# Moving work around the first attention head, the block norms and the first output projection in a hybrid state-space and attention layer

## The chip, the cores and the metric

The kernel runs on one core of a Trainium2 chip (trn2) as one launch. The metric is the device time of that launch in microseconds, the median of several runs. Beside it one execution was taken by the hardware profiler; its instruction trace is what the views below are read from.

The core has a matrix engine (TensorE; PE in the profile, its weight loads PEld), a vector engine (VectorE; DVE), an activation engine (ScalarE; ACT), a general one (GpSimd; POOL), and SyncE (SP), which here only issues DMAs. Each works through its own queue in order.

## The reference

One layer of a streaming encoder on 2048 tokens of width 1024, in float32. One RMS norm feeds one input projection, whose columns go to a state-space layer (512) and to attention (queries, keys, values, 8 heads of 64).

```python
h = rmsnorm(x, norm_mix_g)
proj = h @ w_in
y_ssm = s5_mixer(u_ssm, ...)              # diagonal complex scan, GELU, sigmoid gate
y_att = chunked_attention(q, k, v, bias)  # 64-token chunks, 8 chunks to the left
mixed = concat(rmsnorm(y_ssm, g_ssm), rmsnorm(y_att, g_att))
x = x + mixed @ w_out
h2 = rmsnorm(x, norm_ffn_g)
x = x + (silu(h2 @ w_gate) * (h2 @ w_up)) @ w_down
return rmsnorm(x, norm_final_g)
```

## The kernel before

Everything is kept transposed, features on the 128 partitions and tokens along the free dimension, in four token blocks (`sb`) of 512. Matmuls that must be exact are done with operands split into a high and a low part (`split`, L151: ACT copies the high part, DVE subtracts it for the low one), three matmuls for one product (`mm3`, L145).

The stages follow each other: the state-space input projection (`u_phase`, L398), with the prologue that builds the state-space matrices (`ssm_prologue`, L156) worked in between; attention with the state-space scan woven in (`att_phase`, L687); the mixing stage with the gate, the two norms and the output projection (`mix_phase`, L986); then gate and up, and down, which the change does not touch.

**What sets the order.** TensorE's instructions are issued in the order in which the program writes them (`Ordered`, L69). All other engines' instructions, and the DMAs on SP, are put in order ahead of time by the framework's scheduler: of the instructions whose inputs and buffers are ready in its own model of time, the one that stands earlier in the program goes first, so work can be placed far ahead of its position. At run time each queue is then fixed and in order. A new tile in a rotating buffer waits for the last reader of the tile before it.

**The prologue's end.** The last part of the prologue (`transposes`, L287) turns the state-space input matrices: per group of four, 8 TensorE transposes into tiles `pp`, four ACT copies (L293) and one store on POOL's queue to `bsts` (L296), in two steps each; four groups make eight steps. The list `PRO` (L44) says how many of these steps run behind each step of the first query and key projection (L928 to L930). Behind it, the weights of the first value projection are loaded and split (`next(v0)`, L932), what is left of the prologue runs, and the pools of the attention stage are opened, on the memory of the prologue's pool.

**Queries and keys.** `qk_unit` (L749) projects the queries (`c == 0`) and the keys (`c == 1`) of a pair of heads for one block. For block 0 and pair 0 both are done together (`both`). A head's 64 query rows come out on one half `a` of the partitions (L783). They are wanted on both halves, as a high part `q2h` and a low part `q2l`, because the key tile `k2` holds the key's high part on one half and its low part on the other, so that one matmul over 128 rows does two products. ACT and DVE write half `a` (L786, L787), and two DMAs on SP copy it to half `o` (L788, L789). For the very first pair the tiles are called `hi0x`, `lo0x` (head 0), `hi1x`, `lo1x` (head 1), `hi2x` and `lo2x` (the two key tiles).

**Attention steps.** There are 128 steps `s`, one for each block, pair, head and query tile `qp` of 128 tokens. Step `s` does the scores (`scores`, L840; TensorE writes the one tile `sc`, and DVE's L866 adds the bias, finds the minimum and frees it; ACT takes the exponential), the transposes of step `s`-2 (`transp`, L872), at a head's end the product with the values, and then one turn of all `Unit`s (L665): the projections of the next block, spread over a range of steps that is given relative to the block's first step `g0`, and the state-space work. A `Unit` may do its first piece `pre` steps early. The bias of a head lies in one of two tiles (`nba`, `nbb`); at `qp == 2` the next head's is loaded (L849).

**The operands of a block's projections.** `hT_unit` (L719) loads the eight 128-row tiles of the block's input (L726; one by one into `xt`, two buffers, or in pairs into `raw`, two buffers, which block 0 uses for weights), multiplies them by gain and inverse root (L744, the norm), and splits them (L745, L746). Tiles 0 to 2 (`DB`) have two sets of operand tiles and are done in steps `HTA`; tiles 3 to 7 have one set, which the last projection of the block before reads, and are done in steps `HTS`, with two steps of lead (`HTP`).

**The mixing stage's first block.** `w_out` (L1118) is a generator for two of the eight 128-row tiles of the output projection. Its first half multiplies the attention rows (24 matmuls), its second half the state-space rows, then adds the input tile `xt` (two buffers, L1123), stores the result and squares it. In block 0 the attention half is ready first. So the first halves of pairs 0 and 1 (`held`, L1203) are run ahead, one on either side of `spread` (L1206), which brings the inverse root `no` of the state-space rows onto the partitions by four transposes; their second halves and whole pairs follow (L1213). Between them stand the next block's norms, the sums behind pair 1, the spread and products behind pair 2 (L1223). The projection's results take PSUM tiles `big`, four of them.

Of the kernel before, what the change touches and what calls it, by code (L numbers as in the profile page):

```python
# [18 lines left out]
KT = D // P  # L19
# [18 lines left out]
SGB = 2  # L38
RA1, RA2 = 2, 12
QS = 4, 5, 6, 7, 0, 1, 2, 3  # L40
HTA = -12, -9
HTS = -8, -6
HTP = 2
PRO = 0, 0, 2, 2, 2, 2, 0, 0, 0  # L44
LIGHT = 0.8
SL = 1
LPH = 2
# [639 lines left out]
def att_phase(k, ident, S, aw, x0, roots):  # L687

    tc, nc, io, pfs = k.tc, k.nc, k.io, k.pfs
    with ExitStack() as cx:  # L690
# [28 lines left out]
        def hT_unit(sb, q0=0, q1=KT):  # L719
            hi, lo = hT.setdefault(sb, ([], []))  # L720
            ts = slice(sb * SB, (sb + 1) * SB)
            xts = {}

            def load(q, n=1):
                t = k.t(aw, "raw", [P, 1024], bufs=2) if n > 1 else k.t(aw, "xt", [P, SB], bufs=XB)
                nc.sync.dma_start(t[:].rearrange("p (q t) -> p q t", q=n), io["xt"][q * P : (q + n) * P, ts].rearrange("(q p) t -> p q t", p=P))  # L726
                for m in range(n):
                    xts[q + m] = t[:, m * SB : (m + 1) * SB]

            if q0 == 0:  # L730
                load(0)
                load(1)
            else:
                load(q0)
                for q in range(q0 + 1, q1, 2):
                    load(q, 2)
            for q in range(q0, q1):
                yield
                if q0 == 0 and q + 2 < q1:
                    load(q + 2)  # L740
                xt = xts[q]
                for v, n in zip(hT[sb], ("hi", "lo")):
                    v.append(k.t(aw, f"{n}{q}x" if q < DB and sb % 2 else f"{n}{q}", [P, SB], F32R)[:])
                nc.vector.scalar_tensor_tensor(xt, xt, k.gm[:, q : q + 1], S["rsn"][:, ts], op0=ALU.mult, op1=ALU.mult)  # L744
                nc.scalar.copy(hi[q], xt)  # L745
                nc.vector.tensor_tensor(lo[q], xt, f32(hi[q]), op=ALU.subtract)  # L746
            yield

        def qk_unit(sb, pr):  # L749
            ws = yield from load_ws(sb, (pr, 4 + pr))  # L750
            yield
            hi, lo = hT[sb]
            if (sb, pr) == (0, 0):
                ts = [[k.t(aw, f"{n}{q}x", [P, SB], F32R) for n, q in (("hi", hh), ("lo", hh), (("hi", "lo")[hh], 2))] for hh in range(2)]
            else:
                ts = [(k.t(aa, "q2h", [P, SB], F32R, bufs=3), k.t(aa, "q2l", [P, SB], F32R, bufs=3), k.t(aa, "k2", [P, 2 * SB], F32R, bufs=3)) for _ in range(2)]
            qk[sb, pr] = ts
            if sb > 0:
                for hh in range(2):
                    nc.sync.dma_start(f32(ts[hh][2][:, :SB]), S["k"][(sb - 1) % 2, 2 * pr + hh])  # L760
            both = (sb, pr) == (0, 0)
            pss = []
            for c in range(2):
                if c == 0 or not both:
                    cc = range(2) if both else (c,)
                    pss += [k.t(pfs, "pf", [P, 512]) for _ in cc]
                    for q in range(KT):
                        cs = slice(q * P, (q + 1) * P)
                        for m in cc:
                            wh, wl = ws[m]  # L770
                            mm3(k.ta, pss[m][:], wh[:, cs], wl[:, cs], hi[q], lo[q], q == 0, q == KT - 1)
                            if q == 2:
                                keep_w(4 * m + pr)
                        if q < KT - 1:
                            yield
                ps = pss[c]
                if sb == 0:
                    t = k.t(aa, "yt", [P, SB]) if pr else k.t(aw, "xt", [P, SB], bufs=XB)
                    nc.vector.tensor_tensor(t[:], ps[:], S["rsn"][:, :SB], op=ALU.mult)
                    ps = t  # L780
                for hh in range(2):
                    q2h, q2l, k2 = ts[hh]
                    a = slice(hh * 64, hh * 64 + 64)  # L783
                    o = slice(64 - hh * 64, 128 - hh * 64)
                    if c == 0:
                        nc.scalar.activation(q2h[a, :], ps[a, :], AF.Copy, scale=-0.125)  # L786
                        nc.vector.scalar_tensor_tensor(q2l[a, :], ps[a, :], -0.125, f32(q2h[a, :]), op0=ALU.mult, op1=ALU.subtract)  # L787
                        nc.sync.dma_start(f32(q2h[o, :]), f32(q2h[a, :]))  # L788
                        nc.sync.dma_start(f32(q2l[o, :]), f32(q2l[a, :]))  # L789
                    else:  # L790
                        nc.scalar.copy(k2[a, -SB:], ps[a, :])
                        nc.vector.tensor_tensor(k2[o, -SB:], ps[a, :], f32(k2[a, -SB:]), op=ALU.subtract)
                        if sb < NSB - 1:
                            nc.sync.dma_start(S["k"][sb % 2, 2 * pr + hh], f32(k2[:, -SB:]))
                yield
# [44 lines left out]
        def scores(st):  # L840
            sb, pr, hh, qp = st
            h = 2 * pr + hh
            if qp == 0:
                hd = st_head[sb, h] = Head()
                hd.nb = nbs.pop(h) if nbs else load_nb(h)
                hd.s = {}
                hd.p = None
            hd = st_head[sb, h]
            if qp == 2 and (sb, h) < (NSB - 1, H - 1):  # L849
                nbs[(h + 1) % H] = load_nb((h + 1) % H)  # L850
            q2h, q2l, k2 = qk[sb, pr][hh]
            k0 = max(qp, 4) if sb == 0 else qp
            nk = (qp + 5 - k0) * P
            half = nk // 2 if nk > 512 else nk
            nch = nk // half
            ps = k.t(psum2, "sc", [P, 2, 512])
            for c in range(nch):
                c0 = k0 * P + c * half + k2.shape[1] - 2 * SB
                cols = slice(c0, c0 + half)
                for n, q2 in ((0, q2h), (1, q2l)):  # L860
                    k.ta.matmul(ps[:, c, :half], q2[:, qp * P : (qp + 1) * P], k2[:, cols], start=n == 0, stop=n == 1)
            s = k.t(aa, "s", [P, 640], bufs=3)
            mn = k.t(aa, "mn", [P, 1], bufs=4)
            if (hh, qp) == (0, 0):
                sums[sb, pr] = k.t(aa, "sm", [P, 2, 4], bufs=3)
            nc.vector.tensor_tensor_reduce(  # L866
                s[:, :nk].rearrange("p (a b) -> p a b", a=nch), ps[:, :nch, :half],
                hd.nb[:, nk - 1 :: -1].rearrange("p (a b) -> p a b", a=nch), 1.0, 3e38, ALU.add, ALU.min, mn[:])
            nc.scalar.activation(s[:, :nk], s[:, :nk], AF.Exp, bias=mn[:], scale=-1.0, accum_out=sums[sb, pr][:, hh, qp : qp + 1])  # L869
            hd.s[qp] = s, k0  # L870
# [54 lines left out]
        pro = yield  # L925
        pps = k.pro_psum = tc.alloc_tile_pool(name="apro", bufs=6, space=bass.MemoryType.PSUM, reuse_waits="tile")
        next(pro)
        for n, _ in enumerate(first):  # L928
            for _ in range(PRO[n]):
                next(pro, None)  # L930
        v0 = v_unit(0, 0)
        next(v0)  # L932
        for _ in pro:
# [6 lines left out]
        sp = tc.alloc_tile_pool(name="ssm", reuse_waits="tile", bufs=1)  # L940
        psum = cx.enter_context(tc.tile_pool(name="aps", bufs=1, space=bass.MemoryType.PSUM, reuse_waits="tile"))
        psum2 = cx.enter_context(tc.tile_pool(name="aps2", bufs=1, space=bass.MemoryType.PSUM, reuse_waits="tile"))
        units = []
        for sb in range(NSB):
            g0 = sb * 32
            C = CUT if sb < NSB - 1 else CUTL
            if sb > 0:
                if DB:
                    units.append(Unit(hT_unit(sb, 0, DB), 2 + DB, g0 + HTA[0], g0 + HTA[1], 2))
                units += [Unit(hT_unit(sb, DB), 2 + KT - DB, g0 + HTS[0], g0 + HTS[1], HTP), Unit(qk_unit(sb, 0), QK_N, g0 + C[0], g0 + C[1], 3, light=LIGHT)]  # L950
            units.append(Unit(v_unit(sb, 0), V_N, g0 + C[1], g0 + C[2], 2, light=LIGHT) if sb else Unit(v0, V_N, *V0, done=1))
            for gen, n, c in ((qk_unit(sb, 1), QK_N, 2), (qk_unit(sb, 2), QK_N, 3), (v_unit(sb, 1), V_N, 4), (qk_unit(sb, 3), QK_N, 5)):
                units.append(Unit(gen, n, g0 + C[c], g0 + C[c + 1], 2, light=LIGHT) if sb else Unit(gen, n + 1, C[c], C[c + 1], 4, light=LIGHT, mid=2))
# [32 lines left out]
def mix_phase(k, S, bank):  # L986
# [3 lines left out]
    with ExitStack() as cx:  # L990
# [207 lines left out]
        for sb in range(NSB):  # L1198
# [1 line left out]
                b.m = {}  # L1200
                mixed(b, 0)
            if sb == 0:
                held = [w_out(0, b, 2 * n) for n in range(2)]  # L1203
                next(held[0])
                ps = big()
                spread(k, te, ps[:, :512], b.o[1], 0)  # L1206
                with tc.high_priority():
                    rstd2(b, 1, ps[:, :512])
                    mixed(b, 1)
                next(held[1])  # L1210
            else:
                mixed(b, 1)
            for n in range(4):  # L1213
                if n == 0 and 0 < sb < NSB - 1:
                    nxt = next_block(sb + 1)
                if sb or n > 1:
                    for _ in w_out(sb, b, 2 * n):
                        pass
                else:
                    next(held[n])  # L1220
# [516 lines left out]
```

## Time and profile before

| what | value |
|---|---|
| median of 3 runs | 2264.99 us (2262.37 to 2267.28) |
| the profiled execution | 2267.91 us |
| its span, first to last instruction | 2266.1 us |
| TensorE busy | 2165.6 us (96%) |
| VectorE busy | 1542.4 us (68%) |
| ScalarE busy | 1003.3 us (44%) |
| GpSimd busy | 351.2 us (15%) |
| mean granted TensorE clock | 0.982 |

A line of a timeline gives start and length in us, engine (SPq is SP's queue), source line, operation, out<-in by tile names, shapes, how many were merged, and in brackets the idle time before it and what ended it. The table of waits gives for a line and what it waited for the total, the number of times and the longest. The table of stretches gives for each stretch the busy time and number of instructions of each engine and the TensorE clock that was granted. A source view gives shortest, median and longest duration in ns, and the first and last start. Stages can be told by tile names: `sc`, `pt`, `pj` and `pf` belong to attention (from 138 us on), `big` to the mixing stage (from 720 us on).

### The profile page before, as it was taken

What the parts mean: (1) busy time and instruction counts of PE and PEld (TensorE: products, weight loads), DVE (VectorE), ACT (ScalarE), POOL (GpSimd) and SP (SyncE); (2) the same over time, 40 slices, a digit from 0 to 9 for tenths busy, and PEclk for the clock granted to TensorE, in tenths of its full rate; (3) what the DMA queues carried; (4) which work ended last, traced back from release to release, by engine and by line L of the source; (5) the groups of instructions that cost most, each with busy time, mean ns of one, the idle gap of its engine ahead of it and who ended that gap; (6) DMA issues with size and microseconds to landing.
All of it is one profiled execution on the core that took longest, in us unless ns stands there. A gap on an engine that the chain in (4) does not pass through costs nothing.

```text
span 2266.1 us, 30134 instructions
## 1 busy us (share of the span) xinstructions
PE 2165.6 (96%) x10632; PEld 1825.8 (81%) x10632; DVE 1542.4 (68%) x2695; ACT 1003.3 (44%) x1656; POOL 351.2 (15%) x827
## 2 busy tenths in 40 slices
PE   8988899999997899999999999999999999999997
PEld 6777788898986788778888887888888778888886
DVE  7756666556557756776766668766656477688776
ACT  5445555556557442353333335333333443353322
POOL 2246576656500000000000000000000010000000
PEclk9999999999998899999999999999999999999999
DMA  8878876666552435754556457645433395465652
GB/s 276 254 244 261 268 233 207 192 190 205 187 168 100 138 109 188 251 168 144 180 176 209 162 198 269 199 163 190 140 97 112 102 385 182 167 227 181 216 183 75
DMA packets 194903, 430.41 MB, mean 190 GB/s; under 512 B 19904, under 2 KB 38384, under 8 KB 187648
## 3 DMA queue, kind: packets, MB, share of 16 engines
q1 hardware_dynamic: 187104, 403.58, 53.8%
q0 software_dynamic: 7648, 24.92, 3.6%
q8 instruction: 83, 1.36, 0.2%
q14 instruction: 68, 0.56, 0.1%
HBM read 288.95 MB, written 131.10 MB: 185 GB/s over the span
## 4 chain that ended last, share of the span: by engine, by line
PE 78%; DMA 7%; DVE 6%; ACT 3%; issue 2%; SPq 0%; DVEq 0%; ACTq 0%
PE X L76 20%; PE ps L76 17%; PE Y L76 10%; PE pf L76 10%; PE big L76 6%; PE W L76 5%; PE pj L76 4%; PE pt L79 2%; PE sc L76 2%; DMA acc<-x 2%; DMA lo<-hc 1%; DMA xt<-in_xt 1%; DVE lo L153 1%; DMA hc<-gh 1%; DVE ptl L885 1%
## 5 line engine op out<-in xcount | busy, mean ns | idle before, releaser
L76 PE MATMUL X<-hi,c 128*128 128x512 f32 x1408 | 450.8, 391 | 7.4 <-DVE c L153 5.1
L76 PE MATMUL ps<-hd,hd 128*128 128x512 f32 (+1 forms) x1968 | 429.6, 380 | 3.0 <-DVE hd L153 2.0
L76 PEld LDWEIGHTS ps<-hd,hd 128*128 128x128 f32 x1968 | 357.5, 189 | 73.6 <-DVE hd L153 2.7
L76 PEld LDWEIGHTS X<-hi,c 128*128 128x128 f32 x1408 | 265.1, 188 | 64.1 <-DVE c L153 6.0
L76 PE MATMUL X<-lo,c 128*128 128x512 f32 x704 | 274.6, 390 | 0.0
L153 ACT CAST hd<-hd 128x1536 fp32r<-128x1536 f32 (+1 forms) x106 | 147.5, 1394 | 232.5 <-DMA hd<-hq 170.9
L76 PE MATMUL Y<-hi,c 128*128 128x512 f32 x704 | 226.0, 392 | 3.8 <-DVE c L153 2.3
L153 DVE TENSOR_TENSOR hd<-hd 128x1536 fp32r<-128x1536 f32 (+1 forms) x106 | 174.1, 1644 | 36.2 <-ACT hd L153 35.8
L153 DVE TENSOR_TENSOR c<-S,c 128x512 fp32r<-128x512 f32 x176 | 121.0, 688 | 103.6 <-ACT c L153 103.3
L1516 POOL DMA_DIRECT2D hd<-hq x7 | 5.3, 755 | 1173.2 <-PE X L76 1161.5
L1408 ACT COPY u<-X 128x512 f32<-128x512 f32 x132 | 77.4, 587 | 199.9 <-PE X L76 199.9
L153 ACT CAST c<-S 128x512 fp32r<-128x512 f32 x176 | 109.5, 622 | 122.5 <-PE Y L76 63.8
L76 PE MATMUL big<-m,woh 128*128 128x512 f32 x512 | 162.6, 399 | 0.0
L76 PEld LDWEIGHTS Y<-hi,c 128*128 128x128 f32 x704 | 133.3, 189 | 32.4 <-DVE c L153 2.8
L1550 DVE TENSOR_TENSOR acc<-acc,ps 128x512 f32<-128x512 f32 x196 | 130.2, 682 | 41.6 <-PE ps L76 41.3
L76 PEld LDWEIGHTS X<-lo,c 128*128 128x128 f32 x704 | 132.6, 188 | 27.4
L76 PE MATMUL pf<-hi,w 128*128 128x512 f32 x416 | 149.1, 410 | 0.0
L153 ACT CAST c<-raw 128x512 fp32r<-128x512 f32 x132 | 82.2, 622 | 149.1 <-PE Y L76 69.1
L76 PE MATMUL Y<-lo,c 128*128 128x512 f32 x352 | 137.7, 391 | 0.0
L885 DVE TENSOR_TENSOR ptl<-pt,pth 128x640 fp32r<-128x640 f32 (+3 forms) x152 | 98.3, 647 | 56.1 <-ACT pth L884 54.7
L869 ACT ACTIVATE s<-s,mn 128x640 f32<-128x640 f32 (+4 forms) x128 | 98.0, 765 | 64.1 <-DVE mn L866 58.1
L884 ACT CAST pth<-pt 128x640 fp32r<-128x640 f32 (+3 forms) x152 | 83.8, 551 | 85.6 <-PE pt L79 80.9
(448 smaller groups left out, 4274.1 us busy)
## 6 DMA issues: line engine op xcount, KB each, us to landing
w<-wss SPq DMA_DIRECT2D x36, 1024.0 KB, 6.2
hq<-g SPq DMA_DIRECT2D x140, 256.0 KB, 2.1
hd<-hq SPq DMA_DIRECT2D x35, 768.0 KB, 4.4
hd<-wc SPq DMA_DIRECT2D x35, 768.0 KB, 6.0
raw<-in_w_gate SPq DMA_DIRECT2D x44, 512.0 KB, 3.7
raw<-in_w_up SPq DMA_DIRECT2D x44, 512.0 KB, 4.2
wc<-px SPq DMA_DIRECT2D x66, 256.0 KB, 3.1
wss<-w SPq DMA_DIRECT2D x12, 1024.0 KB, 6.5
```

The costliest lines, as they stand in the source:

```text
L76: return self.tc.keep_in_program_order(self.tc.nc.tensor.matmul(*a, **b))
L79: return self.tc.keep_in_program_order(self.tc.nc.tensor.transpose(*a, **b))
L153: return nc.scalar.copy(hi, raw), nc.vector.tensor_tensor(lo, raw, f32(hi), op=ALU.subtract)
L869: nc.scalar.activation(s[:, :nk], s[:, :nk], AF.Exp, bias=mn[:], scale=-1.0, accum_out=sums[sb, pr][:, hh, qp : qp + 1])
L884: nc.scalar.copy(pth[:, a:b, qp, :], pt[:, a:b, :])
L885: nc.vector.tensor_tensor(ptl[:, a:b, qp, :], pt[:, a:b, :], f32(pth[:, a:b, qp, :]), op=ALU.subtract)
L1408: nc.scalar.copy(u[:], ps[:])
L1516: (nc.gpsimd if aside else nc.sync).dma_start(f32(lo), src.rearrange("g p c -> p g c"))
L1550: V.tensor_tensor(a, a, ps[:], op=ALU.add)
```

## The change

It has four parts.

1. The prologue's transposes are no longer run between the steps of the first query and key projection, but all behind it and behind `next(v0)` (`PRO` goes). For the first head of the first pair, ACT and DVE write the query's high and low parts to both halves, and the two DMAs of that head go.
2. The next head's bias is loaded at `qp == 1` instead of `qp == 2`.
3. `hT_unit` for tiles 3 to 7 loads and norms all five first and splits afterwards. It becomes two units over one generator: loads and norms in steps -13 to -8 before the block (with one step of lead), splits in -8 to -6 with no lead. Tiles 0 to 2 move from -12..-9 to -16..-13.
4. In the mixing stage's first block, three attention halves are run ahead, two before `spread` and one behind it, instead of one and one.

```diff
-HTA = -12, -9
+HTA = -16, -13
 HTS = -8, -6
-HTP = 2
-PRO = 0, 0, 2, 2, 2, 2, 0, 0, 0
+HTN = -13, -8
...
+            def norm(q):
+                nc.vector.scalar_tensor_tensor(xts[q], xts[q], k.gm[:, q : q + 1], S["rsn"][:, ts], op0=ALU.mult, op1=ALU.mult)
+
             if q0 == 0:
                 load(0)
                 load(1)
...
                 load(q0)
                 for q in range(q0 + 1, q1, 2):
                     load(q, 2)
+                for q in range(q0, q1):
+                    yield
+                    norm(q)
             for q in range(q0, q1):
                 yield
-                if q0 == 0 and q + 2 < q1:
-                    load(q + 2)
-                xt = xts[q]
+                if q0 == 0:
+                    if q + 2 < q1:
+                        load(q + 2)
+                    norm(q)
...
-                nc.vector.scalar_tensor_tensor(xt, xt, k.gm[:, q : q + 1], S["rsn"][:, ts], op0=ALU.mult, op1=ALU.mult)
-                nc.scalar.copy(hi[q], xt)
-                nc.vector.tensor_tensor(lo[q], xt, f32(hi[q]), op=ALU.subtract)
+                nc.scalar.copy(hi[q], xts[q])
+                nc.vector.tensor_tensor(lo[q], xts[q], f32(hi[q]), op=ALU.subtract)
...
                     if c == 0:
-                        nc.scalar.activation(q2h[a, :], ps[a, :], AF.Copy, scale=-0.125)
-                        nc.vector.scalar_tensor_tensor(q2l[a, :], ps[a, :], -0.125, f32(q2h[a, :]), op0=ALU.mult, op1=ALU.subtract)
-                        nc.sync.dma_start(f32(q2h[o, :]), f32(q2h[a, :]))
-                        nc.sync.dma_start(f32(q2l[o, :]), f32(q2l[a, :]))
+                        ways = (a, o) if both and hh == 0 else (a,)
+                        for w in ways:
+                            nc.scalar.activation(q2h[w, :], ps[a, :], AF.Copy, scale=-0.125)
+                            nc.vector.scalar_tensor_tensor(q2l[w, :], ps[a, :], -0.125, f32(q2h[a, :]), op0=ALU.mult, op1=ALU.subtract)
+                        if len(ways) == 1:
+                            nc.sync.dma_start(f32(q2h[o, :]), f32(q2h[a, :]))
+                            nc.sync.dma_start(f32(q2l[o, :]), f32(q2l[a, :]))
...
-            if qp == 2 and (sb, h) < (NSB - 1, H - 1):
+            if qp == 1 and (sb, h) < (NSB - 1, H - 1):
...
-        for n, _ in enumerate(first):
-            for _ in range(PRO[n]):
-                next(pro, None)
+        for _ in first:
+            pass
...
+        hts = {sb: hT_unit(sb, DB) for sb in range(1, NSB)}
...
-                units += [Unit(hT_unit(sb, DB), 2 + KT - DB, g0 + HTS[0], g0 + HTS[1], HTP), Unit(qk_unit(sb, 0), QK_N, g0 + C[0], g0 + C[1], 3, light=LIGHT)]
+                units += [Unit(islice(hts[sb], 1 + KT - DB), 1 + KT - DB, g0 + HTN[0], g0 + HTN[1], 1), Unit(hts[sb], 1 + KT - DB, g0 + HTS[0], g0 + HTS[1]), Unit(qk_unit(sb, 0), QK_N, g0 + C[0], g0 + C[1], 3, light=LIGHT)]
...
-                held = [w_out(0, b, 2 * n) for n in range(2)]
+                held = [w_out(0, b, 2 * n) for n in range(3)]
                 next(held[0])
+                next(held[1])
                 ps = big()
                 spread(k, te, ps[:, :512], b.o[1], 0)
                 with tc.high_priority():
                     rstd2(b, 1, ps[:, :512])
                     mixed(b, 1)
-                next(held[1])
+                next(held[2])
...
-                if sb or n > 1:
+                if sb or n > 2:
```

## The prediction

> **What bounds the kernel now.** First the page: TensorE is busy 96% of the span, so only its idle 100 us can be won.
>
> ```profile
> span 2266.1 us, 30134 instructions
> PE 2165.6 (96%) x10632; PEld 1825.8 (81%) x10632; DVE 1542.4 (68%) x2695; ACT 1003.3 (44%) x1656; POOL 351.2 (15%) x827
> ```
>
> Second, the table of whom TensorE waited for (us in total, times, longest). Five rows hold 48 of these 100 us; the parts of the change lie beside four of them.
>
> ```profile
> PE pt L79 <- DVE ptl L885: 21.8, 10, 6.4
> PE sc L76 <- DVE mn L866: 8.0, 4, 5.8
> PE big L79 <- DVE no L110: 7.9, 1, 7.9
> ...
> PE sc L76 <- DMA hi0x<-hi0x: 6.3, 1, 6.3
> ...
> PE sc L76 <- DVE k L792: 4.1, 1, 4.1
> ```
>
> Third, the table by stretches around those waits: start and end, length, busy time of PE, PEld, DVE, ACT and POOL, then the granted TensorE clock, DMA share and GB/s.
>
> ```profile
> 138.00:143.00 5.00, 4.95 (x24) 4.99 (x25) 0.30 (x2) 0.49 (x2) 4.22 (x19) 0.54 1.01 349
> 188.00:194.70 6.70, 0.90 (x4) 0.38 (x3) 5.16 (x9) 3.67 (x6) 6.07 (x18) 0.94 1.01 386
> 194.70:201.00 6.30, 6.26 (x28) 6.25 (x29) 1.43 (x5) 1.65 (x6) 5.60 (x13) 0.53 1.00 383
> ...
> 385.30:389.00 3.70, 3.70 (x13) 3.28 (x14) 3.17 (x6) 2.02 (x4) 3.60 (x5) 0.58 0.53 181
> 738.00:745.80 7.80, 0.00 (x0) 0.00 (x0) 7.33 (x19) 5.11 (x8) 0.00 (x0) 0.63 0.50 138
> 745.80:751.00 5.20, 5.17 (x16) 4.29 (x17) 5.09 (x9) 4.83 (x8) 0.00 (x0) 0.58 1.05 301
> ```
>
> Behind each long wait TensorE works for some microseconds at a clock between 0.53 and 0.58. Length times missing clock is lost: 2.3 us behind the first head (5.0 x 0.46), 3.0 behind 194.7 (6.3 x 0.47), 1.6 behind 385.3, 2.2 behind 745.8. A wait that goes may take this tail along.
>
> **Part 1: the first head.** The timelines of TensorE and of the engines that prepare the first score:
>
> ```profile
> 121.16 1.03 PE L79 MATMUL pp<-ident,wt 128*128 128x128 f32 x8
> 121.58 1.20 ACT L293 COPY v<-pp 128x256 f32<-128x256 f32 x4 [3.74 <-PE pp L79]
> 121.95 0.48 PE L76 MATMUL pf<-hi,w 128*128 128x512 f32 x1
> ...
> 129.87 0.59 POOL L296 DMA_DIRECT2D bsts<-small  x1 [1.24 <-ACT small L293]
> ...
> 132.04 0.63 ACT L786 ACTIVATE hi0x<-xt 64x512 fp32r<-64x512 f32 x1
> 133.50 0.78 DVE L787 SCALAR_TENSOR_TENSOR lo0x<-xt,hi0x 64x512 fp32r<-64x512 f32 x1
> 135.03 0.70 DVE L792 TENSOR_TENSOR hi2x<-xt,hi2x 64x512 fp32r<-64x512 f32 x1
> 138.05 0.44 PE L76 MATMUL sc<-hi2x,hi0x 128*128 128x128 f32 x1 [6.32 <-DMA hi0x<-hi0x]
> ```
>
> Eight transposes lengthen the projection by 0.79 us (121.16 to 121.95). Four such groups leave it, so it ends 3.2 us earlier. They come back, all 32, in the idle stretch that the first score's operands hold open anyway. Of these operands the last that an engine makes is the key's low half, done at 135.73 (135.03 + 0.70). One more activation (0.63 on ACT, beside DVE) and one more subtract (0.78 on DVE) ahead of it make that 136.5; 3.2 us earlier it is 133.3. The two transfers of this head, whose landing ended the wait at 138.05, are gone; the second head keeps its own, with a whole head to land. So 138.05 - 133.3 = 4.8 us are on offer, and the tail of 2.3.
>
> Against it stands ACT. The 16 copies of the transposes (4 in 1.20) need 4.8 us. If all queue behind the evacuations (four activations of 0.63 from 132.04, now five, 3.2 us earlier: until 132.0), TensorE, which needs the copies for free banks and may not pass its transposes, starts the score at about 136.8: 1.2 us gained. The lower end goes to -1: the last store of the transposes, issued at 129.87 now, comes 3 us or more later, and the pools opened behind the prologue take over its memory, so a first score may wait for it. I take **4.5**, 3.5 of the wait and 1.0 of the tail (range -1 to 7.1), nearer to the DVE row, because copies can fill ACT's waits for DVE.
>
> [...]
>
> **Part 2: the bias rows one step earlier.** The timelines of SP, DVE and TensorE at the fourth head:
>
> ```profile
> 185.42 1.07 SPq L695 DMA_DIRECT2D raw<-in_w_v  x2
> 186.53 0.48 SPq L549 DMA_DIRECT2D nbb<-nbs  x1
> ...
> 192.02 2.36 DVE L153 TENSOR_TENSOR w<-raw,w 128x1024 fp32r<-128x1024 f32 x2 [0.27 <-ACT w L153]
> 194.30 0.28 DVE L866 CUSTOM_DVE_ANT_0 s<-sc,nbb 128x128 f32<-128x128 f32 x1
> 194.74 0.55 PE L76 MATMUL sc<-k,q2h 128*128 128x256 f32 x1 [5.84 <-DVE mn L866]
> ```
>
> This head's rows are issued behind two weight loads while DMA is at 1.01, and its first score reduction stands on DVE behind 2.36 us of weight splitting. One step earlier they are ahead of those loads in the program; SP then issues the loads two issues (about 1 us) later. On offer: 5.84 and the 3.0 of tail. But behind that score TensorE needs the very weights that DVE split until 194.4, so much of the wait would only change its name. I take **2.5** (0 to 8.8).
>
> **Part 3: norms ahead, copies later.** From the source views of the norm, the subtract and the loads:
>
> ```profile
> L744 DVE SCALAR_TENSOR_TENSOR raw<-raw,g_mix,rsn x12: 742/747/2144, 241.9 to 398.8; 128x512 f32<-128x512 f32 x12
> ...
> L746 DVE TENSOR_TENSOR lo<-raw,hi x12: 682/690/1539, 243.5 to 533.5; 128x512 fp32r<-128x512 f32 x12
> ...
>   DMA xt<-in_xt: 5.4, 4
> ...
> DMA to landing us min/median/max: 3.5/6.7/8.6
> ```
>
> And the timelines at two heads' starts:
>
> ```profile
> 235.18 1.38 SPq L726 DMA_DIRECT2D raw<-in_xt  x2
> ...
> 237.37 0.45 SPq L566 DMA_DIRECT2D Bst<-bsts  x1
> ...
> 245.65 0.77 PE L76 MATMUL pj<-U,Bst 128*128 128x256 f32 x1 [4.04 <-DMA Bst<-bsts]
> ...
> 381.49 2.99 DVE L746 TENSOR_TENSOR lo<-raw,hi 128x512 fp32r<-128x512 f32 x2
> 384.51 0.68 DVE L792 TENSOR_TENSOR k<-pf,k 64x512 fp32r<-64x512 f32 x1
> 385.25 0.64 PE L76 MATMUL sc<-k,q2h 128*128 128x320 f32 x1 [4.08 <-DVE k L792]
> ```
>
> No instruction is added. In each of three blocks five norms (0.75 each) and six loads move to earlier steps, and so does the work on the first three tiles. At 381.49 two subtracts of the next block's operands (2.99) stand ahead of the key that the next score waits for. With their two steps of lead gone the key is first in the program: I take **4.0** of 4.08 + 1.6 (0 to 5.7). The five subtracts then behind it (3.5 us at 0.69) lie beside scores and the projection's first three tiles, which are double-buffered; without that cover they cost their 3.5. At 235.18 the tile loads stand right ahead of Bst on SP. Moved up they no longer compete with it, if their buffers, which hold weights until then, are free: **2.0** of 4.04 (0 to 4.0). Elsewhere nothing: the last norm already runs at 398.8 while its subtracts run until 533.5, so the fixed order of the engines other than TensorE has them far ahead. The wait that is added is DVE's for these loads; score reductions are queued behind it, and TensorE waits for those.
>
> Every such move reshuffles DVE, ACT and SP. For new waits out of that I take **-3.5** (-14 to 3): about two thirds of the 5.4 us that DVE waits for loads now, the low end at two thirds of the 21.8 us row.
>
> **Part 4: three attention halves.** TensorE's timeline, and a piece of the chain of work:
>
> ```profile
> 745.83 1.09 PE L79 MATMUL big<-ident,no 128*128 128x128 f32 x4 [7.93 <-DVE no L110]
> ...
> 764.73 0.95 PE L76 MATMUL big<-ones,sq 128*128 128x1 f32 x8
> ```
> ```profile
> 780.49 44.54 PE big L76 x200
> ```
>
> TensorE waits 7.93 us for the root `no`, which comes late among DVE work (7.33 busy of 7.80) that the change does not touch. A half product is 24 matmuls of 44.54/200 = 0.223, 5.35 us; one more of them now moves into the wait. It reads the same left operands as the half before and other columns of the same weights, so it can start. The spread still begins at 745.8, and the third half covers the gains and splits that the second covered. Late next may be the following norm: between its sums (764.73) and its spread lies half a product (5.4) instead of a whole one, and roots are computed between other DVE work; I price that at 0 to 2. The third pair's input tile shares two buffers, so its load waits for the first pair's store; two halves (10.7 us) cover it (8.6 at most). The tail of 2.2 I leave, since 2.5 us stay idle. I take **5.5** (3.5 to 7.7).
>
> **Sum:** 4.5 + 2.5 + 4.0 + 2.0 + 5.5 - 3.5 = 15.0. The profiled execution took 2267.9 (the span of 2266.1 and 1.8 around it), so 2252.9; it lies 2.9 above the median of the runs, 2265.0, so **2250**.
>
> **Rivals.** (a) *The first head gains nothing*: ACT's copies pace the transposes, or the first scores wait for the later stores. For it: DMA at 1.01 there, 4.8 us of copies. Against: DVE is idle nearly throughout 138 to 143 (0.30 busy), so a late reduction has slack. 2250 + 4.5 = 2254.5.
>
> (b) *The attention blocks gain nothing*: the fixed order had hoisted the work, and waits change place. For it: 398.8 against 533.5. Parts 1 and 4 less 3.5 remain, 6.5: 2258.5.
>
> (c) *Slower*, by DVE's queue in the attention blocks, whose steps this row of the bias tile's source view times (the second head's first score to the last one, 123 steps):
>
> ```profile
> L866 DVE CUSTOM_DVE_ANT_0 s<-sc,nbb x64: 278/824/826, 158.5 to 708.1; 128x640 f32<-128x640 f32 x48, 128x128 f32<-128x128 f32 x4, 128x256 f32<-128x256 f32 x4, 128x384 f32<-128x384 f32 x4
> ```
>
> A step takes 549.6/123 = 4.5 us. If in each block an earlier norm stands ahead of a score and waits there for a load just issued (8.6 at most), a step hides 4.5, TensorE loses 4.1 and a tail of 3.0, and this happens twice a block: 3 x 14.2 = 43; with one such wait a block, 21. Parts 1 and 4 give back 10, the rest is lost: 2265 + 21 - 10 = 2276 for one. It decides from 3.3 us lost per block. Against it: such waits sum to 5.4 now.
>
> (d) *The third half trades one wait for another* (the second spread waits what the first no longer does), and the order eats the rest: 2264.
>
> **Chances.** Forecast (2241 to 2258) 0.50; (a) 0.15; (b) 0.15, a third of it within 0.2%; (c) 0.12, of it 0.01 within; (d) 0.08. 0.2% is 4.5 us, about what a measurement of this kernel can tell from no change. So faster 0.75, same 0.14, slower 0.11. The range: 2236 with parts 1, 3 and 4 near their upper ends and part 2 at 4; 2266 with parts 1 and 4 at their lower ends and 3.5 lost in the order. It leaves out (c) and a little below.
>
> **What would show it.** Part 1: the first score starts 3 us or more sooner after its projection, with no transfer as releaser, and the clock behind it is above 0.54. Part 2: the fourth head's wait short, or ended by a weight. Part 3: no wait for the key near 385, none for Bst near 245. Part 4: a wait for `no` of about 2.5 us. Wrong would be: new waits over 5 us in the blocks, DVE idle for an input load ahead of scores, or a wait at the second spread.

## The result, and the profile after

| | before | after |
|---|---|---|
| median (22 runs each, same chip) | 2263.24 us | 2265.27 us |
| lowest to highest | 2256.03 to 2268.69 | 2260.30 to 2273.46 |
| profiled execution | 2267.91 us | 2266.11 us |

The ratio of after to before is 1.0008, 95% interval 0.9999 to 1.0016: no difference that can be told, where 15 us were forecast. Executions of one kernel lie up to 8 us from their median, so one profile says where time went, and the medians say how much.

On the page, and then in the table of TensorE's waits (us in total, times, longest), the kernel after reads:

```profile
span 2264.3 us, 30126 instructions
PE 2167.7 (96%) x10632; PEld 1826.7 (81%) x10632; DVE 1544.4 (68%) x2696; ACT 1003.6 (44%) x1657; POOL 353.5 (16%) x827
```
```profile
PE pt L78 <- DVE ptl L893: 21.2, 10, 6.4
PE sc L75 <- DVE mn L874: 12.7, 6, 6.4
PE sc L75 <- DVE k L800: 7.6, 2, 4.9
...
PE big L78 <- DVE no L109: 2.7, 1, 2.7
PE pp L78 <- ACT v L292: 2.7, 1, 2.7
...
PE pf L75 <- ACT w L152: 2.2, 1, 2.2
...
PE pj L75 <- DMA Bst<-bsts: 1.5, 1, 1.5
...
PE pf L75 <- DVE w L152: 1.2, 1, 1.2
```

The wait for the query's transfer (6.3) is gone and the one for `no` fell from 7.9 to 2.7. But the waits for a score reduction (`mn`) grew from 8.0 to 12.7, and three rows are new: for the transposes' copies (`pp`) and twice for the value weights (`pf` <- `w`). The key's row, from 4.1 to 7.6, overstates its growth: 2.74 of it is a wait near 247 us that stands in the table of before as 2.2 us without a releaser. So the key's two waits grew by 1.3 us.

```profile
PE sc L76 <- issue: 2.2, 1, 2.2
```

Where this sits in time is read from the timeline of after (start, length, engine, line, operation; in brackets the idle time before it and what ended it). The groups are the first head, the fourth head, the key near 390, Bst, and the mixing stage:

```profile
131.23 2.31 ACT L292 COPY v<-pp 128x256 f32<-128x256 f32 x8
131.66 4.03 PE L78 MATMUL pp<-ident,wt 128*128 128x128 f32 x20 [2.65 <-ACT v L292]
135.98 0.33 PE L75 MATMUL sc<-hi2x,hi0x 128*128 128x128 f32 x1 [0.30 <-ACT small L292]
139.98 1.18 POOL L295 DMA_DIRECT2D bsts<-v  x2
145.38 0.29 DVE L874 CUSTOM_DVE_ANT_0 s<-sc,nba 128x128 f32<-128x128 f32 x1 [6.81 <-DMA bsts<-v]
145.73 0.58 PE L75 MATMUL sc<-hi2x,hi0x 128*128 128x256 f32 x1 [6.39 <-DVE mn L874]
...
196.80 0.55 PE L75 MATMUL sc<-k,q2h 128*128 128x256 f32 x1 [3.33 <-DVE mn L874]
199.55 1.99 ACT L152 CAST w<-raw 128x1024 fp32r<-128x1024 f32 x2
200.65 0.58 PE L75 MATMUL pf<-w,hi 128*128 128x256 f32 x1 [2.23 <-ACT w L152]
202.43 0.58 PE L75 MATMUL pf<-w,hi 128*128 128x256 f32 x1 [1.20 <-DVE w L152]
...
388.33 2.98 DVE L751 TENSOR_TENSOR lo<-raw,hi 128x512 fp32r<-128x512 f32 x2
391.35 0.68 DVE L800 TENSOR_TENSOR k<-pf,k 64x512 fp32r<-64x512 f32 x1
392.09 0.63 PE L75 MATMUL sc<-k,q2h 128*128 128x320 f32 x1 [4.86 <-DVE k L800]
...
252.61 1.75 PE L75 MATMUL pj<-U,Bst 128*128 128x256 f32 x7 [1.55 <-DMA Bst<-bsts]
...
752.21 0.62 PE L78 MATMUL big<-ident,no 128*128 128x128 f32 x4 [2.67 <-DVE no L109]
```

The first score is still computed 2.1 us earlier than before (135.98 against 138.05), though later than the key's low half allowed: behind the transposes it waits for ScalarE's last copies of them. VectorE may not reduce it until 145.4: it waits for the store of a transposed tile, which GpSimd issues at 139.98 although ScalarE's copies into both tiles `v` are done by 133.5 (131.23 + 2.31). TensorE then waits 6.39 us for the reduction.

Measured on the score reductions, step by step, after lies behind before by 6.6 us at the first, 3.9 at the second head, 4.6 within the third, 2.1 at the fourth head's start, 6.2 two steps on, and 6.0 at the last. On TensorE's instructions of the same number it lies 6.0 behind at 733 us and 0.9 ahead at 870: the mixing stage gives 6.9 back, and little changes on the whole behind it (1.7 ahead at the end). So in this pair of executions after is the shorter one, by 1.8 us, while the medians have it 2.0 longer: before's lies 4.7 us above its median, after's 0.8.

Executions also drift apart ahead of the change. Counted from one of the last matmuls ahead of it (118 us), the first score comes 1.6 to 2.1 us earlier in after and in the eight experiments below with part 1, and between 0.5 earlier and 0.4 later in the three that leave the first head alone. The lags called "from 118 us" below are counted so.

### The profile page after: what moved, and what is told of

It is laid out like the page before. It is cut to its first block, busy times and chain, and to the rows that moved or that the text cites. A ratio compares the mean times of both kernels' runs of the same rounds, so it can differ in the third digit from the quotient of the medians.

```text
span 2264.3 us, 30126 instructions
## 1 busy us (share of the span) xinstructions
PE 2167.7 (96%) x10632; PEld 1826.7 (81%) x10632; DVE 1544.4 (68%) x2696; ACT 1003.6 (44%) x1657; POOL 353.5 (16%) x827
## 4 chain that ended last, share of the span: by engine, by line
PE 77%; DMA 7%; DVE 6%; issue 3%; ACT 3%; POOL 1%; SPq 0%; DVEq 0%; ACTq 0%; POOLq 0%
PE X L75 21%; PE ps L75 16%; PE Y L75 10%; PE pf L75 10%; PE big L75 6%; PE W L75 5%; PE pj L75 4%; PE pt L78 2%; PE sc L75 2%; DMA acc<-x 2%; DMA lo<-hc 1%; DMA x<-xt 1%; DMA xt<-in_xt 0%; DVE ptl L893 0%; ACT hi L152 0%
```

## The experiments

Theory: parts 1 to 3 take their waits away and open others of the same size, each on the queue of an engine that stands behind the one named; part 4 does what it says. Rivals: the parts are harmless and the difference is one of execution; or the projection and the lowered clock (0.50 from 131.6 to 135.0 us in after) cost the time. Each kernel below has its median beside the kernel before on the same chip.

| run | median | ratio, 95% interval |
|---|---|---|
| e1_part1 | 2267.23 | 1.0019 (1.0008 to 1.0029) |
| e2_part2 | 2265.15 | 1.0008 (0.9997 to 1.0019) |
| e3_part3 | 2267.46 | 1.0020 (1.0006 to 1.0034) |
| e4_part4 | 2259.62 | 0.9984 (0.9975 to 0.9993) |
| e5_sp_stores | 2259.68 | 0.9979 (0.9966 to 0.9992) |
| e6_sp_key | 2255.82 | 0.9966 (0.9955 to 0.9977) |
| e7_query_only | 2263.28 | 0.9995 (0.9984 to 1.0006) |
| e8_first_and_mixing | 2256.45 | 0.9967 (0.9958 to 0.9977) |
| e9_key_without_2_3 | 2255.77 | 0.9965 (0.9950 to 0.9979) |
| e10_with_normalizations | 2253.99 | 0.9958 (0.9945 to 0.9971) |
| e11_with_bias_row | 2260.19 | 0.9988 (0.9976 to 1.0000) |
| e12_value_weights_earlier | 2258.65 | 0.9977 (0.9967 to 0.9987) |

Before had medians of 2263.82 (e1 to e4), 2263.97 (e5 to e8) and 2262.66 (e9 to e12). The ratio is not exactly the quotient of the two medians. The kernels have 10 to 12 runs each, e9 has 8 and e10 has 5.

**Each part alone, on the kernel before.** e1, the transposes behind the projection and the query written by engines:

```diff
-        for n, _ in enumerate(first):
-            for _ in range(PRO[n]):
-                next(pro, None)
+        for _ in first:
+            pass
...
+                        ways = (a, o) if both and hh == 0 else (a,)
```

> Part 1 alone on the kernel before (transposes behind the projection, the first head's query written to both halves by engines). Theory: the loss at the first head is part 1's own. POOL issues the four stores of the transposes behind its whole chain of powers, and the first score reduction waits for such a store, because its tile lies in the prologue's memory: first reduction at about 145 us, TensorE idle for about 6.4 us before the second score, the last attention step 4 to 6 us later than in the kernel before, and the time 3 to 6 us longer. Rival: the order that parts 2 and 3 bring about puts the stores there: then the first reduction comes before 139 us and attention ends about 2 us earlier.

4.3 us slower (0.0019 x 2264). The first reduction is at 144.2 us, as expected. The last attention step lies 2.1 us behind before (3.7 from 118 us), where 4 to 6 were expected. Its table of waits has the row of the whole change again:

```profile
PE sc L76 <- DVE mn L869: 14.6, 5, 6.5
```

e2, the bias row one step earlier:

```diff
-            if qp == 2 and (sb, h) < (NSB - 1, H - 1):
+            if qp == 1 and (sb, h) < (NSB - 1, H - 1):
```

> Part 2 alone (the next head's bias loaded at the second query tile). Theory: the fourth head's wait of 5.8 us shrinks, and a wait for the value weights behind it takes most of the place: last attention step within 1.5 us of the kernel before, time the same. Rival, the prediction's term: 2.5 us earlier, with the wait at the fourth head under 1 us and none for weights.

No gain (ratio 1.0008). The timeline of the fourth head says why:

```profile
190.22 0.36 PE L76 MATMUL sc<-k,q2h 128*128 128x256 f32 x1 [3.33 <-DVE mn L866]
192.68 1.99 ACT L153 CAST w<-raw 128x1024 fp32r<-128x1024 f32 x2
193.42 1.06 POOL L609 TENSOR_TENSOR fx<-X,a 128x434 f32<-128x434 f32 x1
193.76 3.78 DVE L153 TENSOR_TENSOR w<-raw,w 128x1024 fp32r<-128x1024 f32 x2 [0.39 <-ACT w L153]
193.78 0.58 PE L76 MATMUL pf<-w,hi 128*128 128x256 f32 x1 [2.65 <-ACT w L153]
194.55 1.90 POOL L610 TENSOR_TENSOR X<-X,fx 128x434 f32<-128x434 f32 x1
195.61 0.58 PE L76 MATMUL pf<-w,hi 128*128 128x256 f32 x1 [1.24 <-DVE w L153]
```

The wait at the fourth head falls by 2.5 us, from 5.84 to 3.33. But the softmax now goes ahead of the value weights' casts on ScalarE, and TensorE waits 2.65 and 1.24 for these. The same work was hidden in the 5.84 before.

e3, the normalizations in steps of their own:

```diff
-HTA = -12, -9
+HTA = -16, -13
...
-HTP = 2
+HTN = -13, -8
...
+                for q in range(q0, q1):
+                    yield
+                    norm(q)
```

> Part 3 alone (norms ahead, splits without lead). Theory: the order of VectorE is set by what is ready first, not by the place in the program, so the two subtracts still stand ahead of the key at the third block and that wait stays at 4 to 5 us; the wait for Bst shrinks from 4.0 to about 1.5, and small waits give it back: last attention step within 2 us of the kernel before, time the same. Rival, the prediction's terms: 6 us earlier, no wait for the key.

4.5 us slower by its ratio, and the key's wait is what it was (timeline of e3; before: 4.08):

```profile
246.48 3.56 PE L76 MATMUL pj<-U,Bst 128*128 128x256 f32 x8 [2.76 <-DMA U<-u]
...
381.60 2.98 DVE L752 TENSOR_TENSOR lo<-raw,hi 128x512 fp32r<-128x512 f32 x2
384.61 0.68 DVE L798 TENSOR_TENSOR k<-pf,k 64x512 fp32r<-64x512 f32 x1
385.35 0.41 PE L76 MATMUL sc<-k,q2h 128*128 128x320 f32 x1 [4.07 <-DVE k L798]
```

The two subtractions still stand ahead of the key, and Bst's wait fell from 4.04 to 2.76 with U in its place. The same time was expected. Its score reductions run within 2.1 us of before's up to 669 us. But before's execution lies 4.1 us above the median of e1 to e4, this one 1.0 above its own, so the pair cannot show 4.5 us, and they stay open.

e4, three attention halves:

```diff
-                held = [w_out(0, b, 2 * n) for n in range(2)]
+                held = [w_out(0, b, 2 * n) for n in range(3)]
                 next(held[0])
+                next(held[1])
...
```

> Part 4 alone (three attention halves ahead). Theory: it gains what it gained in the changed kernel, 5.3 us of waiting and some of the clock's tail, 5 to 7 us over the mixing stage, whatever happens ahead of it: time 2256 to 2259 where the kernel before takes 2263. Rival: the gain is given back later, since the time of the changed kernel did not move: then the mixing stage ends 5 us earlier and the whole is the same.

3.6 us faster (1.6 to 5.7 by the interval), at the weak end of what was expected. The wait in its timeline, and the stretch behind it in its table by stretches (busy PE, PEld, DVE, ACT, POOL, then the granted clock):

```profile
743.32 0.62 PE L79 MATMUL big<-ident,no 128*128 128x128 f32 x4 [2.22 <-DVE no L110]
```
```profile
741.10:746.30 5.20, 2.98 (x17) 2.57 (x17) 4.96 (x11) 3.40 (x6) 0.00 (x0) 1.00 0.96 287
```

Here even the clock's tail is gone: 1.00, where before had 0.58 behind this wait. The four effects sum to +0.0031 (each within 0.0009 to 0.0014), against +0.0008 for the whole; without e3's, which stays open, to +0.0011.

**What in part 1 costs.** e5 is the whole change with one word changed:

```diff
-            nc.gpsimd.dma_start(S["bst"][b_], bst.rearrange("p g c n -> p (g c n)"))
+            nc.sync.dma_start(S["bst"][b_], bst.rearrange("p g c n -> p (g c n)"))
```

> The changed kernel with one word changed: the four stores of the transposed state inputs (bsts) are issued by SP instead of GpSimd. Theory: in the changed kernel the copies of the first transposes are done at about 133 us, but their stores stand on GpSimd's queue behind its chain of powers and are issued from 140.0 on; the first score reduction waits until 145.4 for the first one to land, because it writes memory that the stored tile still holds. Issued by SP they leave at about 133 to 135 and land by 138 to 139: first reduction at 138.0 to 139.5 us, TensorE's 6.39 us wait at its second score tile falls under 2 us, the end of the attention stage lies 4 to 7 us earlier than in the changed kernel, time 2258 to 2261. Rival: the evacuation of the transposes (2.65 us of waiting for ScalarE's copies) and the lower clock behind it set the first head, or another tile's store does: first reduction at 143 us or later, time 2264 to 2267.

Measured: 2259.68, and the ratio goes from 1.0008 to 0.9979. Its timeline:

```profile
132.53 1.38 SPq L295 DMA_DIRECT2D bsts<-v  x2
...
139.54 0.29 DVE L874 CUSTOM_DVE_ANT_0 s<-sc,nba 128x128 f32<-128x128 f32 x1 [2.90 <-DMA bsts<-v]
139.90 0.38 PE L75 MATMUL sc<-hi2x,hi0x 128*128 128x256 f32 x1 [2.37 <-DVE mn L874]
```

The stores leave 7.4 us earlier (1.7 of it because this execution runs ahead from 118 us on) and TensorE's wait falls from 6.39 to 2.37. That GpSimd's queue held them is shown; a memory wait of 2.4 us stays even so (under 2 was expected). The time fell, with intervals that do not meet. This trace does not carry the gain to the end of attention, which was expected 4 to 7 us earlier than in the change: its last step lies 6.3 us behind before, that of the change 6.0. Its wait for Bst is 3.49 against 1.55, and from 118 us the lead of 4.0 us at the second head is down to 1.0 by step 110 of 128.

e7 leaves the transposes where they were and keeps only the engine-written query:

```diff
+                        ways = (a, o) if both and hh == 0 else (a,)
```

> The kernel before with only the first head's query written to both halves by the engines; the transposes stay among the projection's columns. Theory: the 6.32 us wait for the query's half (DMA hi0x) falls to 3 us or less, since the transposes' copies are long done, and no store is late: first reduction at 135 to 136.5 us (138.8 before), end of attention 1.5 to 3.5 us earlier, time 2259 to 2262. Rival: the two additional writes stand ahead of the key's own casts and subtractions on ScalarE and VectorE, or the gain is waited away at the fourth head, whose bias row lands at a time of its own: end of attention within 1 us of before, time 2263 to 2265.

Measured: no gain that can be told (0.9995), by the rival's first half. The first reduction came at 137.57, later than expected. From its timeline:

```profile
135.80 0.45 PE L76 MATMUL sc<-hi2x,hi0x 128*128 128x128 f32 x1 [4.85 <-DVE hi2x L795]
```

The transfer's 6.32 us become 4.85 us for the key's low half, which now stands behind three query writes on VectorE.

**What the key waits for.** e6 is e5 with VectorE's order pinned:

```diff
-                nc.vector.tensor_tensor(lo[q], xts[q], f32(hi[q]), op=ALU.subtract)
+                ins = nc.vector.tensor_tensor(lo[q], xts[q], f32(hi[q]), op=ALU.subtract)
+                if q0 and sb > 1:
+                    k.tc.keep_in_program_order(ins)
```

and likewise for the key's subtraction from the second block on.

> The kernel of e5_sp_stores, and VectorE's subtraction that forms the key's low half is kept in the order of the program, ahead of the next block's low halves. Theory on the third part: moving the normalizations earlier left the wait for the key because four subtractions of the next block (1.5 us each there) still stand ahead of the key's subtraction on VectorE. With the order kept, TensorE's wait for k at the start of the third block (4.86 us in the changed kernel) falls to 2.5 us or less, and the one at 244 us (2.74) to 1 us or less; time 2 to 4 us below e5_sp_stores. Rival: the key comes late from TensorE and ScalarE (its projection ends late), or something behind it is late next: the wait stays above 3.5 us or is taken over by another within 10 us, time within 1.5 us of e5_sp_stores.

Measured: 3.9 us below e5, and the wait at the third block is 1.45 us (4.10 in e5). The smaller one, near 241 us, stayed at 2.75: that half of the expectation failed. The intervals of e5 and e6 overlap (0.9966 to 0.9977).

e8 is before with part 1, SP's stores and part 4 (the diffs of e1, e5 and e4):

> The kernel before with the first part (transposes moved, query by engines), the stores of the transposes on SP, and the three attention halves of the last part; the bias row and the normalizations stay as before. Theory: e4_part4 gained 3.6 us alone (ratio 0.9984), and the first part with its stores on SP is worth 0 to 3 us: 2256 to 2260, below both kernels. Rival: the first part is worth nothing or costs even with the stores moved (the cover that the transposes had among the projection's columns is gone, 2.65 us of waiting and a lower clock): 2260 to 2264.

Measured: 2256.45, as the theory said. It puts the change together: 0.9967 with parts 1 and 4 and SP's stores, 0.9979 with parts 2 and 3 as well (e5), 1.0008 with the stores on GpSimd (the change). The store is 6.6 us of this by the ratios; the wait of 2.65 us for the copies stayed in e5, so the second rival isn't what costs them. At the first head itself the traces agree: from 118 us, the second reduction lies 4.3 us behind before in the change and in e1, and within 0.2 us of before in all seven kernels with SP's stores. So there part 1 costs 4.3 with GpSimd's stores and gains nothing with SP's. By the ratios e8 is still 3.8 us below e4, which lacks part 1; their intervals overlap, and where that would come from stays open.

e9 adds the pinned order of e6 to it, e10 adds part 3 to e9, e11 adds part 2 to e9:

> The kernel of e8_first_and_mixing (first part with SP's stores, three attention halves) and the key's subtraction kept ahead of the next block's low halves on VectorE; neither the earlier bias row nor the earlier normalizations. Theory: what the key waited for was VectorE's order alone, so the wait at the third block falls from 4.09 us to 1 to 2 us without the earlier normalizations: 2.5 to 3 us below e8, a ratio to before of 0.995 to 0.996, about 2252 to 2255. Rival: the order only helps where the normalizations have been moved ahead: the wait stays above 3 us and the time that of e8.

> The kernel of e9_key_without_2_3 plus the third part (normalizations in units of their own, ahead). e3_part3 alone was 4.5 us slower than before, and its trace shows no wait of that size. Theory: moving them gives nothing, since the order on VectorE decides, and costs the waits that it opened (0.6 us more at the second block, a wait for U): 0 to 2 us above e9. Rival: the 4.5 us are a real cost of it: 3 to 6 us above e9. Second rival: with the key's order kept it helps at last: 1 to 3 us below e9.

> The kernel of e9_key_without_2_3 plus the second part (the next head's bias row loaded a step earlier). Theory: the wait at the fourth head falls from 5.9 to 3.3 us, and then the value projection waits 2.6 and 1.5 us for the split of its weights, whose casts now stand behind the softmax on ScalarE: within 1.5 us of e9. Rival: the second part is worth its 2.5 us once nothing else disturbs it: 2 to 3 us below e9.

In e9 the theory fell. The timeline of e9, then that of e10:

```profile
381.04 2.99 DVE L746 TENSOR_TENSOR lo<-raw,hi 128x512 fp32r<-128x512 f32 x2
384.06 0.68 DVE L797 TENSOR_TENSOR k<-pf,k 64x512 fp32r<-64x512 f32 x1
...
384.80 0.42 PE L76 MATMUL sc<-k,q2h 128*128 128x320 f32 x1 [4.09 <-DVE k L797]
```
```profile
381.47 0.68 DVE L803 TENSOR_TENSOR k<-pf,k 64x512 fp32r<-64x512 f32 x1 [1.25 <-ACT k L802]
...
382.21 0.42 PE L76 MATMUL sc<-k,q2h 128*128 128x320 f32 x1 [1.45 <-DVE k L803]
...
386.98 3.17 DVE L752 TENSOR_TENSOR lo<-raw,hi 128x512 fp32r<-128x512 f32 x2
```

Pinned to the program's order without part 3, the subtractions are ahead of the key all the same: the program itself has them there, two steps of lead ahead. Part 3 alone moves them in the program, and the scheduler pulls them forward again (e3). Only both together put the key first, 2.6 us in this wait. TensorE then waits 0.68 and 0.48 us for subtractions that now run behind the key, and 0.61 for a reduction, which takes most of that back. In time e10 is 1.8 us below e9, their intervals overlapping. Nothing here has a lower median, and its interval lies below both kernels of the change. No 4.5 us of cost appears with part 3 in it.

e11's median is 4.4 us above e9's, with the fourth head's wait at 3.33 and the value weights' at 2.24 and 1.21. Neutral was expected of part 2. A loss isn't settled: the two intervals overlap (0.9976 to 0.9979), and the two profiled executions are equally long (2257.64 and 2257.62). A gain isn't seen.

e12 is e11 with those weights loaded and split two steps earlier:

```diff
-                units.append(Unit(gen, n, g0 + C[c], g0 + C[c + 1], 2, light=LIGHT) if sb else Unit(gen, n + 1, C[c], C[c + 1], 4, light=LIGHT, mid=2))
+                units.append(Unit(gen, n, g0 + C[c], g0 + C[c + 1], 2, light=LIGHT) if sb else Unit(gen, n + 1, C[c], C[c + 1], 6 if c == 4 else 4, light=LIGHT, mid=4 if c == 4 else 2))
```

> The kernel of e11_with_bias_row, and the second value unit of the first block loads its weights two steps earlier (6 ahead of its start in the place of 4) and splits them two steps earlier. Theory: the split is what took back the second part's gain. With the casts ahead of the fourth head's softmax again and the loads landed before, the waits of the value projection fall from 2.6 and 1.5 us to under 1.5 us in sum and that at the fourth head stays at 3.3 us or less: 2 to 4 us below e11. Rival: the buffers of the weights are not free that early, the casts hold up the softmax behind them, and the fourth head waits 5 to 6 us again: within 1 us of e11.

Measured: 1.5 us below e11, still above e9; neither the theory's 2 to 4 nor the rival's 1. The timeline is the rival's:

```profile
188.78 1.99 ACT L153 CAST w<-raw 128x1024 fp32r<-128x1024 f32 x2
189.86 2.49 DVE L153 TENSOR_TENSOR w<-raw,w 128x1024 fp32r<-128x1024 f32 x2 [0.27 <-ACT w L153]
192.27 0.28 DVE L873 CUSTOM_DVE_ANT_0 s<-sc,nbb 128x128 f32<-128x128 f32 x1
192.70 0.55 PE L76 MATMUL sc<-k,q2h 128*128 128x256 f32 x1 [5.96 <-DVE mn L873]
```

The waits for the weights are gone, and the fourth head waits 5.96 again. The rival's first reason does not hold: the loads were issued 10 us earlier than in e2 (173.4 against 183.4) and took 7.6 us at most, so the buffers were free. The casts still ran at 188.8, right behind the key's. In these runs, whichever goes first on ScalarE and VectorE, the split or the reduction, the other is waited for.

## Why the prediction was wrong

- **Part 1, 4.5: the failed step.** The prediction named the store ("a first score may wait for it"), but priced it at -1, as if it were later by the 3 us of the moved transposes. It was on GpSimd's queue, behind a chain of small instructions that builds the powers, and the prediction asked neither about that chain nor about its order: more than 6 us from the copies to the issue (133.5 to 139.98), then the landing. By e1 the term is about -4 in place of 4.5, and by e5 the store is its greatest piece. The choice of VectorE's row over ScalarE's failed too: the key's low half was done at 132.5 (133.3 was worked out), but the first score stood behind ScalarE's copies until 135.98 (136.8 by their row). So 2.1 us were on offer in place of 4.8, and with the stores on SP none of them is left at the second reduction.
- **Part 2, 2.5: right where it was measured, wrong as a gain.** The wait fell by exactly that. "Much of the wait would only change its name" was written, and 2.5 was meant to be what is left after that; 3.9 us came back (e2).
- **Part 3, 4.0 and 2.0: failed.** "With their two steps of lead gone the key is first in the program": so it is, but VectorE's fixed order isn't the program's (e3, e6, e9), and the wait went from 4.08 to 4.86. The same paragraph had found for the norms that the order hoists them. Bst's wait fell (4.04 to 1.55), but the score reductions on both sides of it show TensorE arriving later rather than Bst sooner: between the steps before and behind (241 and 253 us before) only 0.6 us is won.
- **Order, -3.5.** The waits for the weights, 2.23 + 1.20 = 3.4 us, came to that size, but they weren't a random reshuffle: they are what the removed wait had covered. The new 2.65 is ScalarE's copies, which part 1 had considered. The key's two waits grew by 1.3.
- **Part 4, 5.5: right.** 7.93 to 2.67 is 5.3. The second spread does not wait; the sums ahead of it wait 0.60 in place of 0.26 (0 to 2 was priced). By its ratio alone part 4 is worth 3.6 (1.6 to 5.7), less than the 5.5 but inside the range. The tail left out went in e4 (1.00 behind the wait).
- **Rivals.** (a) by its second reason, and (b), held at the same time: 2250 + 4.5 + 8.5 = 2263 on a scale whose start is 2265. They had 0.15 each, and no case had both. The argument against (a), that VectorE is idle there and so a late reduction has slack, overlooked that `sc` is one tile: TensorE waited 6.39 us for the reduction.
- **The clock behind the first head, 1.0 of part 1's 4.5: not won.** From the table by stretches of after:

```profile
131.60:135.00 3.40, 3.34 (x16) 3.35 (x17) 1.51 (x3) 3.29 (x13) 3.09 (x11) 0.50 1.01 360
135.00:138.40 3.40, 3.10 (x26) 2.86 (x25) 1.09 (x1) 2.25 (x5) 2.93 (x10) 1.00 0.87 289
```

TensorE's 16 instructions of the first stretch are all transposes, at a clock of 0.50 behind the wait of 2.65; in the next the clock is back at 1.00. In e12 a stretch at 0.50 from 132.2 on, with TensorE busy for 3.46 of 3.70 us, was followed by 0.50 once more (135.9 to 139.0), so what brings the clock back stays open. The tail itself did not go: behind the new wait of 6.39 us the clock of after is 0.51 from 141.8 to 145.2 and 0.65 from 145.2 to 150.2.

## What to carry to other kernels

Before a wait is taken away, list what the other engines do inside it: that may be late next, and it can be as long as the wait. When work is moved past a point, follow each store that it issues to its queue, its engine's order there, and the memory that someone wants next. And where a scheduler orders an engine by readiness, moving lines in the program may move nothing until the order is pinned, and pinning does nothing until the program has the order wanted.

## What the runs showed of the hardware

- Where subtractions on VectorE and GpSimd's instructions ran side by side, some of both took longer than others of their size. The weights' two subtractions took 2.36 us in before and 3.78 in e2. Beside those of e2, two of GpSimd's 434-wide passes took 1.90 and 1.92, where before's first five, from 197.34 on, took 1.03 to 1.06. In before two of GpSimd's 4-wide instructions beside the subtractions took 1.12 and 1.18, and the next two, at 194.61 and 195.02 with no subtraction beside them, 0.20 and 0.21. Why is not shown.
- A wait of 2.65 us isn't always followed by a lower clock. In after it is (0.50 above); in e10 the same wait, from 128.5 on, is not, as the table by stretches shows:

```profile
128.50:131.20 2.70, 0.05 (x1) 0.05 (x1) 2.66 (x4) 2.62 (x6) 2.56 (x4) 1.00 0.50 164
131.20:135.00 3.80, 2.87 (x20) 1.95 (x20) 1.42 (x3) 3.80 (x15) 3.41 (x12) 1.00 0.99 356
```

So the tail that the prediction put at 2.3 us and priced at 1.0 is there in some traces and not in others: behind a wait of 2.65 us the clock was 0.50 in after and 1.00 in e10. What decides it is not shown.
